# RMS norm and matmul on one core: stores of two tiles from tile 80 on

## The chip, the cores and the metric

One NeuronCore of a Trainium2 chip. The metric is device time in microseconds (us), lower is better. One execution is also taken by the hardware profiler; its trace gives the span from the first to the last instruction.

## The reference: what is computed

```python
batch, seq, dim, out_dim = 16, 1024, 512, 768

def reference(x, gamma, weight, eps):
    rms = np.sqrt(np.mean(x ** 2, axis=-1, keepdims=True) + eps)
    x_norm = x / rms * gamma
    return np.matmul(x_norm, weight).astype(np.float32)
```

All inputs and the output are float32: 16,384 rows of 512 numbers come in (32 MiB), 16,384 rows of 768 go out (48 MiB). Every byte of both has to pass the DMA engines once.

## The kernel before, in words

**Tiles.** The 16,384 rows are cut into `NT` = 128 tiles of 128 rows; a tile has one row on each of the 128 partitions. The main loop takes tiles in pairs `j` (tiles 2j and 2j+1), 64 of them. `gamma` is multiplied into the weights once, which are kept in bf16 (`w_bf`).

**Work on a tile.** GpSimd casts x to bf16 (`cast`, line 188; `cast_quad`, line 260). ScalarE squares each row and sums it (`square`, line 196), takes the root for eight tiles at a time (line 201), and VectorE makes the reciprocal (`rstd`, line 203). PE transposes the tile in words of two bf16 (line 230) and VectorE copies the result out of PSUM (line 239); for 28 of the 128 tiles VectorE transposes 32x32 blocks itself (line 271). PE then multiplies the transposed tile with the weights (line 300), into one of three accumulators in PSUM. `finish_tile` multiplies the accumulator with `rstd` into the output buffer `ot`: ScalarE does even tiles (line 279), VectorE odd ones (line 281).

**Output buffers and stores.** `ot` has three buffers of `OG` = 8 tiles; group g of eight tiles (tiles 8g to 8g+7) uses buffer g % 3. `stretches` gives for every tile the first tile and the size of its store (`o_first`, `o_size`). `store(i)` is called after each tile and issues a DMA on SP's queue only where tile i is the last one of its store (line 293). So a whole group leaves in one DMA of 3 MB, except where `stretches` is told to cut a group: the first one into 1, 1, 2 and 4 tiles, the last but one into 4 and 4, the last into 4, 2 and 2. The output rows are dealt out so that each partition owns neighbouring rows of the output (`rows`): a store of n tiles writes n × 3 KB in one piece from each partition.

**Loads.** x comes in eight tiles at a time (2 MB, 16 KB a partition), into two buffers of 16 tiles. The first 32 tiles are asked for on SP's queue at the start; the rest on ScalarE's queue, one load every four pairs (line 177).

**What sets the order.** The order is written out by hand: every operation is recorded in program order by `Order.add` with the cells that it reads and writes, and `Order.emit` adds the waits from those cells. The cells of `ot` are single tiles, so that the first write to a slot waits for the DMA that last read this slot. In `finish_tile`, the last tile of each store also reads the cell of the tile before it (`before`): VectorE then waits for ScalarE's neighbouring tile, and SP needs to wait for VectorE only.

```python
before = [("ot", s, i % OG - 1)] if i == o_first[i] + o_size[i] - 1 else []
```

Of the kernel before, what the change touches and what calls it, by code (L numbers as in the profile page):

```python
# [100 lines left out]
def kernel(  # L101
# [20 lines left out]
    NT = N // P  # L122
    NP = NT // 2
    XG, OG = 16, 8
    FIRST, START, LEAD = 2 * XG, 4, 14

    def stretches(group, parts):
        first, size, i = {}, {}, 0
        for g in range(NT // group):
            for n in parts.get(g, [group]):  # L130
                for t in range(i, i + n):
                    first[t], size[t] = i, n
                i += n
        return first, size

    last = NT // OG - 1
    x_first, x_size = stretches(OG, {0: [4, 4]})
    o_first, o_size = stretches(OG, {0: [1, 1, 2, 4], last - 1: [4, 4], last: [4, 2, 2]})

    def rows(ap, i, n):  # L140
        base, t = (i - i % OG, OG) if OG <= i < XG else (x_first[i], x_size[i]) if i < OG else (i - i % XG, XG) if i < 2 * XG else (i - i % (2 * XG), 2 * XG)
# [340 lines left out]
```

## Time and profile before

| | us |
|---|---|
| three runs | 208.81, 208.94, 214.95 |
| median | 208.94 |
| profiled execution, its time | 209.01 |
| profiled execution, its span | 207.1 |

DMA issues of the profiled execution (the page's list; bytes and the median time from issue to landing):

```profile
out_dram<-ot SPq DMA_DIRECT2D x13, 3072.0 KB, 22.0
xt<-in_x_dram ACTq DMA_DIRECT2D x12, 2048.0 KB, 19.0
...
out_dram<-ot SPq DMA_DIRECT2D x4, 1536.0 KB, 10.9
out_dram<-ot SPq DMA_DIRECT2D x3, 768.0 KB, 6.7
```

ScalarE's waits (who waited for whom, us in total, times, the longest):

```profile
ACT ot L279 <- PE ps L300: 41.7, 52, 1.9
ACT ot L279 <- DMA out_dram<-ot: 4.2, 3, 1.7
```

How to read the profile: a span is cut into 40 slices, and each digit is the busy share of a slice in tenths (9 is 90% or more). PE is the matmul engine, PEld its weight loads, DVE VectorE, ACT ScalarE, POOL GpSimd, SP the engine that issues stores. The DMA share is the mean over the core's 16 DMA engines. q1 is SP's DMA queue, q10 ScalarE's. A store is split over all 16 DMA engines, eight rows each, and it has landed when the last of the 16 has finished. L279 is line 279 of the kernel.

### The profile page before, as it was taken

How to read it: one execution, taken by the hardware profiler on the slowest of the kernel's cores; microseconds unless marked ns; L12 is line 12 of the kernel's file. 1: busy time of each engine (PE TensorE's matmuls, PEld its weight loads, DVE VectorE, ACT ScalarE, POOL GpSimd, SP SyncE). 2: the span in 40 equal slices, each digit the busy share in tenths (PEclk: the TensorE clock that was granted, in tenths of full speed). 3: DMA queues.
4: the chain of work that ended last, by engine and by line, in shares of the span. 5: the costliest groups of instructions: out<-in, count | busy, mean ns of one | idle time of the engine just before them, and what ended most of it. 6: DMA issues, size and time to landing. Idle time of an engine off the chain costs nothing.

```text
span 207.1 us, 2793 instructions
## 1 busy us (share of the span) xinstructions
PE 196.4 (95%) x1236; PEld 73.1 (35%) x717; DVE 149.4 (72%) x255; ACT 144.6 (70%) x343; POOL 60.0 (29%) x34
## 2 busy tenths in 40 slices
PE   7799999999999999999999999999999999999940
PEld 1233444343344334433333333443344334343310
DVE  0435654999569984999579984999579984999530
ACT  2688899678867787677867877687858768683310
POOL 1437761067003370063403351060702306000000
PEclk9999999999999999999999999999999999999997
DMA  5999999999999999999999999999999999999993
GB/s 208 422 434 449 389 399 418 440 419 432 426 437 435 432 441 419 426 435 432 435 421 427 441 426 427 430 438 424 429 437 426 434 435 435 408 451 387 392 417 125
DMA packets 5920, 85.62 MB, mean 413 GB/s; under 512 B 658, under 2 KB 660, under 8 KB 1556
## 3 DMA queue, kind: packets, MB, share of 16 engines
q1 hardware_dynamic: 4176, 60.29, 68.8%
q10 hardware_dynamic: 1732, 25.17, 28.5%
q8 instruction: 7, 0.11, 0.2%
q14 instruction: 5, 0.04, 0.0%
HBM read 35.13 MB, written 50.33 MB: 413 GB/s over the span
## 4 chain that ended last, share of the span: by engine, by line
PE 92%; DMA 2%; DVE 1%; ACT 1%; issue 0%; SPq 0%
PE ps L300 82%; PE ps L230 10%; DMA xt<-in_x_dram 2%; DVE ot L281 0%; ACT jk L196 0%; DVE xT L239 0%; DVE w_bf L281 0%; ACT rms L201 0%; DVE rstd L203 0%; SPq L477 0%; SPq L436 0%
## 5 line engine op out<-in xcount | busy, mean ns | idle before, releaser
L300 PE MATMUL ps<-w_bf,xT 128*128 128x512 bf16 (+1 forms) x800 | 149.3, 329 | 0.2 <-DVE w_bf L281 0.2
L279 ACT ACTIVATE ot<-ps,rstd 128x768 f32<-128x768 f32 x64 | 57.7, 901 | 47.8 <-PE ps L300 41.7
L196 ACT ACTIVATE jk<-xt 128x512 bf16<-128x512 f32 x128 | 78.7, 618 | 3.1 <-DMA xt<-in_x_dram 3.1
L188 POOL CAST xb<-xt 128x2048 bf16<-128x2048 f32 (+3 forms) x21 | 46.4, 2221 | 113.4 <-PE ps L230 70.1
L281 DVE TENSOR_SCALAR ot<-ps,rstd 128x768 f32<-128x768 f32 x64 | 64.8, 1013 | 8.5 <-PE ps L300 7.8
L296 PEld LDWEIGHTS <-xT 128*128 128x128 bf16 x400 | 39.5, 99 | 60.3 <-issue 52.5
L230 PE MATMUL ps<-ident_f,xb 128*128 128x128 f32 x200 | 54.4, 276 | 1.1 <-POOL xb L188 1.1
L239 DVE COPY xT<-ps 128x1024 bf16<-128x1024 bf16 (+1 forms) x53 | 34.6, 654 | 26.6 <-PE ps L230 24.9
L271 DVE STREAM_TRANSPOSE xTq<-xq 32x256 f32<-32x256 f32 x112 | 48.8, 435 | 3.4
L230 PEld LDWEIGHTS ps<-ident_f,xb 128*128 128x128 f32 x200 | 28.3, 143 | 46.7 <-issue 44.0
L300 PE MATMUL ps<-w_bf,xTq 128*128 128x512 bf16 x224 | 42.8, 326 | 0.0
L196 ACT ACTIVATION_READ_ACCUMULATOR jk<-xt 128x1 f32 x128 | 24.4, 190 | 0.0
L296 PEld LDWEIGHTS <-xTq 128*128 128x128 bf16 x112 | 11.0, 98 | 14.5 <-issue 14.5
L260 POOL CAST xq<-xt 128x2048 bf16<-128x2048 f32 x7 | 13.3, 1897 | 0.0
L203 DVE RECIPROCAL rstd<-rms 128x8 f32<-128x8 f32 (+3 forms) x20 | 3.8, 192 | 7.5 <-ACT rms L201 7.3
L201 ACT ACTIVATE rms<-ssq,eps_sb 128x8 f32<-128x8 f32 (+3 forms) x20 | 6.0, 300 | 0.6
L300 PE MATMUL ps<-warm 128*128 128x512 bf16 x10 | 4.8, 629 | 1.4 <-DVE eps_sb L354 1.4
L279 ACT ACTIVATE w_bf<-w_f,g_sb 128x768 bf16<-128x768 f32 x2 | 1.9, 935 | 1.2 <-DMA w_f<-in_weight_dram 1.2
L377 DVE COPY g_sb<-ps 128x4 f32<-128x4 f32 x1 | 0.2, 163 | 3.2 <-PE ps L371 3.2
L341 ACT ACT_TABLE_LOAD x1 | 1.3, 1283 | 1.5 <-SPq L436 1.5
L281 DVE TENSOR_SCALAR w_bf<-w_f,g_sb 128x512 bf16<-128x512 f32 (+2 forms) x3 | 1.4, 482 | 0.6 <-DMA w_f<-in_weight_dram 0.6
L371 PEld LDWEIGHTS ps<-ident_f,g_row 2*128 2x128 f32 x2 | 0.3, 201 | 2.6 <-issue 2.6
(10 smaller groups left out, 2.0 us busy)
## 6 DMA issues: line engine op xcount, KB each, us to landing
out_dram<-ot SPq DMA_DIRECT2D x13, 3072.0 KB, 22.0
xt<-in_x_dram ACTq DMA_DIRECT2D x12, 2048.0 KB, 19.0
xt<-in_x_dram SPq DMA_DIRECT2D x3, 2048.0 KB, 18.3
out_dram<-ot SPq DMA_DIRECT2D x4, 1536.0 KB, 10.9
out_dram<-ot SPq DMA_DIRECT2D x3, 768.0 KB, 6.7
xt<-in_x_dram SPq DMA_DIRECT2D x2, 1024.0 KB, 7.3
w_f<-in_weight_dram SPq DMA_DIRECT2D x2, 768.0 KB, 7.1
out_dram<-ot SPq DMA_DIRECT2D x2, 384.0 KB, 19.2
```

Of the source, the lines that this page charges most:

```text
L188: run(POOL, lambda: POOL.tensor_copy(out=xb[s][:, i % 8:i % 8 + n, :], in_=src), of, cells("xb", s, i % 8, n))
L196: run(ACT, lambda: ACT.activation(out=jk[j], in_=src[:, 0, :], func=AF.Square, accum_out=ssq[:, i:i + 1]), of, [("jk", j), ("ssq", i)])
L201: run(ACT, lambda: ACT.activation(out=rms[:, s], in_=ssq[:, s], func=AF.Sqrt, scale=1.0 / D, bias=eps_sb), [("ssq", t) for t in range(i, i ...
L203: run(DVE, lambda: DVE.reciprocal(out=rstd[:, s], in_=rms[:, s]), [("rms", i)], [("rstd", t) for t in range(i, i + n)])
L230: run(PE, lambda: PE.transpose(out=tp[b][:, t, h, :], in_=words[:, lo:lo + P], identity=ident_f), cells("xb", s, j % 4 * 2 + t) + ["ident" ...
L239: run(DVE, lambda: DVE.tensor_copy(out=dst[:, t:t + n, :], in_=src[:, t:t + n, :]), [("tp", b)], cells("xT", j % 4, t, n))
L260: run(POOL, lambda: POOL.tensor_copy(out=xq[s], in_=src), of, [("xq", s)])
L271: run(DVE, lambda: DVE.transpose(out=dst, in_=src), [("xq", s)], [("xTq", s)])
L279: run(ACT, lambda: ACT.mul(out=dst, in_=src, mul=r), reads, writes)
L281: run(DVE, lambda: DVE.tensor_single_scalar(out=dst, in_=src, scalar=r, op=mybir.AluOpType.mult), reads, writes)
L296: run(PE, lambda: PE.ldweights(lhsT), [cell])
L300: run(PE, lambda: PE.add_instruction(mybir.InstMatmult(name=nc.get_next_instruction_name(), engine=mybir.EngineType.PE, ins=[PE.lower_ap(r ...
```

## The change

```diff
-    o_first, o_size = stretches(OG, {0: [1, 1, 2, 4], last - 1: [4, 4], last: [4, 2, 2]})
+    o_first, o_size = stretches(OG, {0: [1, 1, 2, 4], **{g: [2, 2, 2, 2] for g in range(NT * 5 // 8 // OG, last + 1)}})
```

`NT * 5 // 8 // OG` is 10 and `last` is 15. So groups 10 to 15 (tiles 80 to 127) are each stored in four DMAs of two tiles, 768 KB, 6 KB a partition: 24 stores. Before, these tiles left in nine stores: groups 10 to 13 whole, group 14 in two of four tiles, group 15 in one of four and two of two. On SP's queue that makes 9 issues of 3 MB and 24 of 768 KB beside the first group's, where it was 13 of 3 MB, 3 of 1.5 MB and 2 of 768 KB. Since each store's last tile waits for the tile before it, every odd tile from 81 on now has that wait, and the waits for free slots of `ot` follow the smaller stores. No other instruction is added, taken away or moved on any engine.

## The prediction

> **What bounds the kernel now.** I read the page's head first: the engines' busy time and the 40 slices.
>
> ```profile
> span 207.1 us, 2793 instructions
> PE 196.4 (95%) x1236; PEld 73.1 (35%) x717; DVE 149.4 (72%) x255; ACT 144.6 (70%) x343; POOL 60.0 (29%) x34
> ...
> DMA  5999999999999999999999999999999999999993
> GB/s 208 422 434 449 389 399 418 440 419 432 426 437 435 432 441 419 426 435 432 435 421 427 441 426 427 430 438 424 429 437 426 434 435 435 408 451 387 392 417 125
> ```
>
> Two resources are full at once: the PE and the 16 DMA engines. So I asked for busy time by stage (columns: stretch; length; busy us and count of PE, PEld, DVE, ACT, POOL; clock; DMA share; GB/s).
>
> ```profile
> 100.00:180.00 80.00, 80.00 (x522) 30.57 (x303) 63.57 (x107) 60.10 (x145) 22.54 (x10) 1.00 1.01 431
> 180.00:190.00 10.00, 10.00 (x67) 3.84 (x38) 9.54 (x18) 5.58 (x14) 0.00 (x0) 1.00 0.99 424
> 190.00:200.00 10.00, 9.11 (x57) 2.64 (x27) 6.08 (x9) 3.60 (x4) 0.00 (x0) 1.00 0.93 390
> 200.00:207.10 7.10, 0.00 (x0) 0.00 (x0) 0.16 (x1) 0.00 (x0) 0.00 (x0) 0.80 0.50 203
> ```
>
> PE never pauses before 198, and from 100 to 180 the DMA engines are full at 431 GB/s. Which ends last? The chain of waits ends with the last VectorE scaling, at 199.15 + 1.02 = 200.17:
>
> ```profile
> 199.15 1.02 DVE ot L281
> ```
>
> That chain follows compute instructions only; the span runs 6.9 us further, to 207.1. The list of DMA issues in the window 200 to 203, and the DMA view of 203 to 207.1, show what fills the rest:
>
> ```profile
> out_dram<-ot SPq DMA_DIRECT2D x1, 768.0 KB, 5.7
> ```
> ```profile
> DMA  6951101010101001010100101000000000000000
> ...
> q1 hardware_dynamic: 45, 0.17, 10.5%
> ```
>
> The last store is issued at 200.46 and lands 5.74 us later, at 206.20, although its 768 KB need under 2 us at 424 GB/s: it queues behind earlier stores. From 203.6 on the digits show one engine in sixteen still moving. In the trace's records of landings, fifteen engines have finished the last store by 204.00 and one finishes at 206.20. This late engine lands the last six stores at 191.22, 195.01, 198.78, 202.50, 204.33 and 206.20. Eight packets of a four-tile store (456 ns each, below) make 3.65 us and those intervals are 3.72 to 3.79, so it hardly rests. **The end is set by the total work of the slowest DMA engine**, plus 0.9 us to the end of the span. The other fifteen are ahead and run dry for moments (0.93 busy in 190 to 200).
>
> **The change, part by part.** Each engine moves 8 of a transfer's 128 rows, one packet a row. Tiles 80 to 127 now leave in 24 stores of 6 KB rows; before it was 9 stores (four of 24 KB rows, three of 12 KB, two of 6 KB). Bytes, loads, and everything before tile 80 stay. PE, VectorE and GpSimd keep their instructions and order.
>
> *More packets.* From the trace's packet records, median length and distance to the next packet of the same engine: 24,576 B take 912 ns, next after 908; 12,288 B 460, next after 456; 6,144 B 234, next after 231. Four 6 KB packets cost 924 where one 24 KB packet cost 908. Per engine:
> - tiles 80 to 111: 4 × 8 × 908 = 29.06 us become 16 × 8 × 231 = 29.57: +0.51
> - tiles 112 to 123: 3 × 8 × 456 = 10.94 become 6 × 8 × 231 = 11.09: +0.14
> - tiles 124 to 127: unchanged
> - 15 more completions, a 4-byte packet of 9 ns each: +0.14
>
> Sum +0.79 us. All of it lies on the path if the late engine never rests, which the change only makes surer, since each pair is issued as soon as it is ready. Lower bound: the late engine needed 7.51 us for the last eight-tile store (0.939 a tile), 0.930 a tile for the last four-tile one and 0.925 for the last two pairs; 44 tiles at 0.925 for 0.94 give −0.6. Upper bound: 6 KB packets in the tail had a mean of 238, not 234; 4 ns on 176 packets add 0.7: +1.5. I take +0.8, the sum over medians, because 6 KB packets beside loads (28 to 42 us) also had a median of 234.
>
> The Trainium skill, page "DMA: Bandwidth & Descriptors", section "Bandwidth", speaks against this change: it asks for at least 1 MiB a DMA, and its table has 341 GB/s there. At that rate a 768 KB store would take 2.3 us (an estimate from the page), and 22 of them for tiles 80 to 123 some 10 us more than now. The trace disagrees where stores queue: the last two pairs land 1.87 us apart, 420 GB/s.
>
> *Issue on SP.* 15 more issues of 0.33 us. SP does nothing else here: it waits for VectorE most of the time (95 us on that one row of its waits). Zero; if several pairs came ready at once the DMA engines would still have a backlog of over 5 us to work on.
>
> *New waits on VectorE.* Every odd tile from 81 now waits for ScalarE's even tile, where only the last of a store did. Queued behind it on VectorE are the 32x32 moves and the PSUM copies that PE needs. ScalarE's scaling ends 0.12 to 1.26 us before VectorE's begins in all but two pairs, 104/105 and 106/107 (−0.08 and 0.01), and there ScalarE itself had waited 1.68 us for a store. Zero; without that cover at most 0.1 us per pair, and PE has three accumulators.
>
> *Buffers and the two queues.* A slot of `ot` is now free when its pair has landed, not its eight. ScalarE waits for stores three times, 4.2 us in all, once 1.69 before tile 96 and once 1.68 before tile 104; the second should vanish. It gains nothing, since PE did not pause there. Against that, loads get ahead: while both queues are full they take turns by packet (36 to 42 us: 16 KB load packets had 55.4% of the engines, 12 KB store packets 43.9%; that is 611 to 460). With 6 KB rows against 16 KB the stores' part falls to 234 / (234 + 611) = 28%. Worst case, loads take everything: small packets come up when the store of tiles 72 to 79 has landed (155.39). Loads still owe the rest of one that lands at 158.04, 2.65 us at 38.6% (their share in 156 to 168) = 1.0, and the last one, 2.10 MB / 431 GB/s = 4.9, so they end at 161.3; tiles 80/81 land near 163.7, 82/83 near 165.5, 84/85 near 167.4. Tiles 104, 106, 108 need them at 165.9 at the earliest, 168 and 170. No one waits: zero. Loads land earlier (the last at 170.47 now), and PE was not waiting for them.
>
> *End.* After the last store all is as before: landing, 0.9 us, end.
>
> **Rivals.**
> - *The late engine catches up.* It is 2.2 us behind the next one at the end, but only 0.2 when the store issued at 143.59 lands; the lag grows while long store packets run. With 6 KB rows it does no worse per tile than the others (0.925 to their 0.93). If growth stops at 0.5, the end moves by 0.8 − 1.7 = −0.9: 208.1. Against: packets of a backlogged engine are where it lost time, whatever their length. Chance 0.15.
> - *6 KB packets are dear when all engines write them.* The top tenth in the tail took 252 to 260 ns. If in the long run of 176 packets that is the rule, +21 ns each add 3.7: 209.0 + 0.8 + 3.7 = 213.5, slower. It decides above some 253 ns a packet (+2%). Against: the medians of 234 in both places where such packets ran. Chance 0.06.
> - *A gap after each store.* If engines paused for each completion, the price is what surrounds a lone transfer: 1.0 us from the first issue to its first packet, 0.5 from the last packet to the landing. 15 × 1.5 = 22: 232. Against: the pairs 1.87 apart leave 0.02 beside 8 × 231. The skill's page puts about 2 us of fixed cost on a DMA (section "Anatomy of one DMA"), of the path issued from GpSimd; here it overlaps. Chance 0.02.
> - *Faster by over 2%* needs 204.8. Compute ends at 200.17; issue at 200.46, then 1.0 to the first packet, 1.85 of packets, 0.5 to land, 0.9, and 1.9 outside the span: 206.6 is the floor without any queue. Only noise gets there: 0.02.
>
> **How the numbers follow.** The profiled execution took 209.01 with a span of 207.1 (1.9 outside it); the median of the three runs is 208.94, so nothing is corrected. Forecast 209.0 + 0.8 = 209.8, chance 0.75 for 208.4 to 210.5 by the bounds. The range takes in the first rival below, and above the beginning of the second: 207.8 to 211.2. Within 2% (204.8 to 213.1, about what a measurement of this kernel can tell from no change) lie the forecast and the first rival: 0.90. Slower 0.08, faster 0.02.
>
> **What would show it.** In the changed profile: more data packets on q1 (tiles 80 to 123 in 22 stores of 128 rows, 2,816, where 7 stores made 896) of about 234 ns; PE full until 198 and the last VectorE scaling within 0.3 us of 200.2; the last load landing some 5 us or more before 170.5; no ScalarE wait before tile 104; the last landing near 207.0, from one late engine. Wrong would be: idle DMA engines before 190, PE pauses after 155, 6 KB packets above 245 ns, or the late engine on time with the rest.

## The result and the profile after

| | before | changed |
|---|---|---|
| median of 12 runs, us | 209.11 | 210.15 |
| ratio (95% interval) | | 1.0047 (1.0029 to 1.0065) |
| profiled execution, its time / span | 209.01 / 207.1 | 210.06 / 208.1 |

The change costs about 1.0 us (0.6 to 1.4), half a per cent. A few executions ran some per cent longer whatever the kernel (214.95 and 213.11 here); the ratios leave them out, and the profile of many_24k below is of such a run, 1.7% above that kernel's fastest. The head of the page of the changed kernel, its 40 slices:

```profile
span 208.1 us, 2803 instructions
...
DMA  5999999999999999999999999999999999999992
GB/s 196 428 435 441 406 385 434 421 437 439 428 433 425 439 433 416 432 435 435 424 430 439 422 430 420 424 427 425 438 390 423 414 421 424 422 425 423 423 426 92
DMA packets 8080, 85.62 MB, mean 411 GB/s; under 512 B 898, under 2 KB 900, under 8 KB 4612
```

The bytes are the same; the last nine full slices lie at 414 to 426 GB/s, where the kernel before went from 451 down to 387 as engines ran dry. Busy time by stage (same columns as before), of the changed kernel twice, then of the kernel before where only its stores of 24 and 12 KB rows run:

```profile
100.00:150.00 50.00, 49.63 (x320) 18.98 (x188) 39.82 (x68) 37.82 (x92) 14.80 (x7) 1.00 1.01 429
```
```profile
165.00:203.00 38.00, 33.24 (x210) 11.71 (x117) 26.54 (x42) 19.95 (x44) 2.94 (x2) 0.99 1.02 424
```
```profile
172.00:190.00 18.00, 18.00 (x120) 7.10 (x70) 14.87 (x26) 11.75 (x28) 2.32 (x2) 1.00 1.00 428
```

Read the last two columns: the engines are full in all three stretches (a share above 1.00 comes from records that overlap: a 6 KB packet is 234 ns long and the next starts after 231). They move 429 GB/s with 24 KB stores and 16 KB loads, and 424 with 6 KB stores alone, where the kernel before moves 428 with longer rows. They are not idle; the same bytes take longer. (PE's 49.63 of 50 is not a pause: the trace holds 1,212 PE records where the same instructions left 1,236 before.)

Loads and stores while both queues are full, 152 to 160 (queue: packets, MB, share of the engines):

```profile
q10 hardware_dynamic: 161, 2.38, 70.2%
q1 hardware_dynamic: 158, 0.96, 28.8%
```

158 packets to 161: the queues take turns packet by packet, so the stores' share falls with their packets, to 28.8%. The last load lands at 163.81, 6.7 us earlier than before, and nobody is faster for it. ScalarE's waits for stores, from its timeline, are these three, before tiles 80, 88 and 96; in the profile before they were before tiles 88, 96 and 104, and the one before tile 104 is gone:

```profile
130.73 0.90 ACT L279 ACTIVATE ot<-ps,rstd 128x768 f32<-128x768 f32 x1 [1.19 <-DMA out_dram<-ot]
...
142.86 0.90 ACT L279 ACTIVATE ot<-ps,rstd 128x768 f32<-128x768 f32 x1 [1.17 <-DMA out_dram<-ot]
...
155.16 0.90 ACT L279 ACTIVATE ot<-ps,rstd 128x768 f32<-128x768 f32 x1 [2.20 <-DMA out_dram<-ot]
```

The end: the last scaling of the chain, the last store (in the list of issues of 200 to 203 it stands with 7.3 us, though it is issued at 199.81), and the DMA view of 204 to 208.1:

```profile
198.49 1.02 DVE ot L281
```
```profile
out_dram<-ot SPq DMA_DIRECT2D x1, 768.0 KB, 7.3
```
```profile
DMA  1422222201101010100101010000000000000000
```

Compute ends 0.65 us earlier than in the trace before (it is ahead by 0.63 at tile 0 already, where nothing was changed), and the last landing comes 0.94 us later, at 207.14. What is late is the DMA engines' work, not the last tile.

### The profile page after: what moved, and what is told of

It is laid out like the page before. It is cut to its first block, busy times and chain, and to the rows that moved or that the text cites. A ratio compares the mean times of both kernels' runs of the same rounds, so it can differ in the third digit from the quotient of the medians.

```text
span 208.1 us, 2803 instructions
## 1 busy us (share of the span) xinstructions
PE 193.4 (93%) x1212; PEld 72.6 (35%) x717; DVE 149.6 (72%) x255; ACT 144.4 (69%) x343; POOL 59.9 (29%) x34
## 4 chain that ended last, share of the span: by engine, by line
PE 90%; DMA 2%; DVE 1%; issue 1%; ACT 1%; SPq 0%
PE ps L300 80%; PE ps L230 10%; DMA xt<-in_x_dram 2%; DVE ot L281 0%; ACT jk L196 0%; DVE xT L239 0%; DVE w_bf L281 0%; ACT rms L201 0%; DVE rstd L203 0%; SPq L477 0%; SPq L436 0%
## 5 line engine op out<-in xcount | busy, mean ns | idle before, releaser
L300 PE MATMUL ps<-w_bf,xT 128*128 128x256 bf16 (+1 forms) x783 | 145.5, 326 | 1.4 <-DVE w_bf L281 0.5
L300 PE MATMUL ps<-w_bf,xTq 128*128 128x256 bf16 (+1 forms) x217 | 41.8, 324 | 0.4
L300 PE MATMUL ps<-warm 128*128 128x512 bf16 x10 | 4.3, 567 | 1.4 <-DVE eps_sb L354 1.4
```

The lines of the kernel that those rows point to most:

```text
L300: run(PE, lambda: PE.add_instruction(mybir.InstMatmult(name=nc.get_next_instruction_name(), engine=mybir.EngineType.PE, ins=[PE.lower_ap(r ...
```

## The experiments

All ratios are against runs of the kernel before on the same chip. For the profiles, the end of the last scaling and the last landing, us:

| kernel | ratio (95%) | last scaling ends | last landing |
|---|---|---|---|
| before, first profile / again | | 200.16 / 200.23 | 206.20 / 206.17 |
| changed, again | 1.0042 (1.0023 to 1.0062) | 200.59 | 206.97 |
| long_6k | 1.0037 (1.0005 to 1.0068) | 201.88 | 206.68 |
| head_pairs | 1.0040 (1.0018 to 1.0063) | 199.93 | 206.75 |
| tail_pairs | 0.9998 (0.9975 to 1.0020) | 200.06 | 206.24 |
| half_pe | 1.0053 (1.0032 to 1.0074) | 197.28 | 208.01 |
| pairs_all | 1.0135 (1.0104 to 1.0167) | 200.21 | 209.34 |
| long_3k_32 | 1.0200 (1.0148 to 1.0252) | 207.71 | 211.76 |
| relief15 | 1.0138 (1.0092 to 1.0185) | 199.97 | 208.26 |
| many_24k | 1.0759 (1.0698 to 1.0820) | 204.60 | 225.10 |

Three theories: *more packets* (the sum of the prediction), *more stores* (a price per store, whatever its packets), *other order* (loads ahead of stores, earlier issue, the new waits).

**long_6k: the packets without the stores.** On the kernel before, a gap (`PAD`) of 16 numbers after every second tile in the buffer:

```diff
-    ot = [sb(f"ot{n}", [P, OG, O], F32) for n in range(3)]
+    ot_flat = [sb(f"ot{n}", [P, (OG // 2) * (2 * O + PAD)], F32) for n in range(3)]
...
+        return buf.rearrange("p (a w) -> p a w", w=2 * O + PAD)[:, t // 2:(t + n) // 2, :2 * O]
...
```

> The nine stores of the kernel before, issued when they were, but the output buffer has a gap of 64 bytes after every second tile from tile 80 on, so that each row leaves in pieces of 6 KB: packets as in the changed kernel, stores and waits as before. Theory 'more packets' (the sum of the prediction): +0.51 and +0.14 us over the kernel before, +0.65, ratio 1.003; the DMA rate falls to about 424 GB/s where only stores run. Rival 'more stores' (each extra store costs the late engine some 0.07 us, whatever its packets): no change, ratio 1.000, 431 GB/s. Rival 'other order' (loads ahead of stores, earlier issue, the new waits on VectorE): loads still get ahead, the waits are gone; no clear change.

Measured: 1.0037, and on one chip a last landing 0.51 after that of before_again (the kernel before, profiled again, below), where the sum says 0.65. From 171 to 189 the engines move 424 GB/s at a share of 1.02, in before_again 430 at 1.00. Nine stores with short packets pay most of the price; 'more stores' at no change falls outside the interval, if narrowly. The waits for stores, here and then in before_again:

```profile
ACT ot L289 <- DMA out_dram<-ot: 11.0, 4, 4.2
...
PE ps L312 <- ACT ot L289: 2.2, 2, 1.9
```
```profile
ACT ot L279 <- DMA out_dram<-ot: 10.2, 4, 3.1
...
PE ps L300 <- ACT ot L279: 0.7, 1, 0.7
```

On this chip the kernel before waits 10.2 us itself, not the 4.2 of its first profile, so the short packets add little to the sum. What they lengthen is the wait before tile 104, from 2.97 to 4.23 us: a slot comes free only when all eight tiles have landed, and the store that frees it now has its short packets beside long loads. PE pauses 2.2 us, and the last scaling ends 1.65 us later than in before_again. The end does not follow: eleven engines land the last store between 205.42 and 205.62, but the slowest, which set the end, are later, up to 206.68.

**many_24k: the stores without the packets.**

```diff
+            parts = n // 2 if first >= 80 else 1
+            for q in range(parts):
+                p0, p1 = P // parts * q, P // parts * (q + 1)
+                order.transfer(SP, lambda p0=p0, p1=p1: SP.dma_start(out=rows(out, first, n)[p0:p1], in_=src[p0:p1]),
+                               reads=cells("ot", s, first % OG, n))
...
```

> The other half alone: 24 stores from tile 80 on with the long packets of before. Each whole group of tiles 80 to 111 leaves in four stores of 32 partitions, each four-tile store in two of 64 partitions, all issued when the one store was. 'More packets': only 15 completions of 9 ns, +0.14 us, ratio 1.001. 'More stores': the whole of the change's cost, +0.8 to +1.0 us, ratio 1.004 to 1.005. A mapping of partitions to engines other than with 128 partitions could add something of its own; then the packets' lengths in the trace tell.

It answers another question. DMA view of 172 to 204, where only such stores run:

```profile
DMA packets 639, 9.56 MB, mean 299 GB/s; under 512 B 196, under 2 KB 196, under 8 KB 196
...
q1 hardware_dynamic: 638, 9.55, 97.4%
```

The engines are busy 97.4% of the time and move 299 GB/s: the packets themselves are slower. In this window those of 24 KB take 1,304 ns in the mean, 916 in the kernel before. The expectation had named that stores of 32 or 64 partitions could do this; why they do is not shown. The Trainium skill, page "SBUF — State Buffer", section "Door 1: The DMA port swizzle", has the reason it would give: 16 ports into the memory, eight partitions each, so that 32 partitions reach only eight of them. The loss of rate agrees; which ports were used no run here shows. As a test of the price per store this run is void.

**pairs_all: the dose.** Groups 1 to 9 in pairs too:

```diff
-    o_first, o_size = stretches(OG, {0: [1, 1, 2, 4], **{g: [2, 2, 2, 2] for g in range(NT * 5 // 8 // OG, last + 1)}})
+    o_first, o_size = stretches(OG, {0: [1, 1, 2, 4], **{g: [2, 2, 2, 2] for g in range(1, last + 1)}})
```

> The change made from tile 8 on: 60 stores of two tiles. 'More packets': for each of the nine more groups 8 x 16 ns and three completions, 0.155 us, so +1.4 on top of the change's 0.8 to 1.0: +2.2 to +2.4 over the kernel before, ratio 1.011. 'More stores' at 0.067 each: 42 more, +2.8, ratio 1.013. 'Other order': with 6 KB against 16 KB rows all along, loads run ahead and stores fall behind early; ScalarE waits for stores more than three times, PE pauses, and the time is more than 4 us longer, ratio above 1.02.

Measured 1.0135, +2.8 us (2.2 to 3.5), last landing 209.34. 'Other order' above 1.02 is excluded; ScalarE waits for stores 6.2 us in all, less than the 10.2 in before_again. Packets and completions give 2.2, the lower edge, so something of the size of 0.6 us remains (by last landings more: 3.17 after before_again, 1.81 of it packets, leaves 1.36). Put on the 42 more stores, 1.36 would be 32 ns each, where the sum has 9, and the number of 'more stores' fits here as well; only the kernels with short packets and unchanged stores speak against it. But the trace has another place for it: the 16 KB load packets, with a median of 611 ns in both, have a mean of 630 here and 618 in before_again, and over 120 of them an engine that is 1.4 us. So a price per store is not shown.

**relief15: does one engine set the end?** On the changed kernel:

```diff
+            cuts = [0, 120, P] if first in (120,) else [0, P]
+            for p0, p1 in zip(cuts, cuts[1:]):
+                order.transfer(SP, lambda p0=p0, p1=p1: SP.dma_start(out=rows(out, first, n)[p0:p1], in_=src[p0:p1]),
+                               reads=cells("ot", s, first % OG, n))
...
```

> The changed kernel, but tiles 120/121 leave in a store of 120 partitions and one of the last 8. The trace tells how many engines each uses; if 120 rows go to 15 engines and 8 rows to 8, one engine has 1.85 us less to do and eight have 0.23 more. If the late engine is the one left out and it alone sets the end: the last landing comes 1.3 us earlier (the next engine is 1.58 ahead of it), 208.7 to 208.9, ratio to the kernel before 0.999. If another engine is the late one: +0.0 to +0.3 against the changed kernel, 210.2 to 210.4. If the end is not set by one engine's work but by the number of stores or by the issue of the last: no gain either, and the sixteen landings of the last store keep their spread of 3.8 us.

The landings show 15 engines on the 120 rows and 8 on the 8, as supposed. But around this store the rate falls, as in many_24k; stretches before it and around it:

```profile
164.00:194.00 30.00, 29.72 (x191) 10.64 (x106) 25.09 (x43) 19.16 (x44) 3.73 (x2) 1.00 1.02 423
195.00:200.00 5.00, 3.91 (x25) 1.07 (x11) 2.04 (x2) 1.80 (x2) 0.00 (x0) 1.00 0.98 358
```

Five microseconds at 358 instead of 423 GB/s are 0.8 us of work more. The kernel is 2.9 us (1.9 to 3.9) above the kernel before, where the changed kernel on this chip is 0.9 above it; the window accounts for only a part. Whether one engine alone sets the end stays open.

**before_again and after_again: two profiles of one chip.**

> The kernel before, profiled on the same chip as the next three, to compare traces of one chip. If the late engine belongs to the kernel, one engine is again some 2 us behind the next at the last store; if it belongs to the chip it was run on, the sixteen landings of the last store have another shape. Time 208.9 to 209.7.

> The changed kernel on the same chip. 'More packets': +0.8 us over the kernel before, ratio 1.003 to 1.005, whether one engine is late or not, with 424 GB/s where only stores run. If the change's cost came from one late engine's dislike of short packets alone, it vanishes where no engine is late: ratio 1.000 to 1.002.

206.97 − 206.17 = 0.80 us between the last landings; the sum was 0.79. That the two agree to 0.01 is luck: the lengths of all packets, a sixteenth of their sum, differ by 0.5 us between the two profiles of the kernel before alone (202.11 and 202.62). When compute starts does not show in the end: tile 0 is scaled 0.73 us later in after_again than in before_again, 0.63 earlier in the first pair, and the last landings are 0.80 and 0.94 apart.

On this chip it is not one engine that is late: in before_again the last store lands on thirteen engines by 204.68 and on the others at 205.51, 205.82 and 206.17. A lone late engine comes and goes with the profile: the slowest is 1.74 us behind the next in head_pairs (another chip) and 1.53 in pairs_all (this chip). What makes it late stays open; the price is about the same with it and without.

**long_3k_32: packets of 3 KB, the stores of before.** As long_6k, with a gap after every tile from tile 32 on:

```diff
-        return buf.rearrange("p (a w) -> p a w", w=2 * O + PAD)[:, t // 2:(t + n) // 2, :2 * O]
+        return buf.rearrange("p (t w) -> p t w", w=O + PAD)[:, t:t + n, :O]
```

> The stores of the kernel before, in number and place, with a gap of 64 bytes after every tile of the output buffer from tile 32 on: rows leave in pieces of 3 KB. A 3,072 B packet's successor comes after 118 ns, so eight cost 944 for 908: 10 groups x 8 x 36 = 2.88 us; three four-tile stores 8 x 16 each, 0.38; two pairs 8 x 5 each, 0.08. 'More packets': +3.3 to +3.5 us, ratio 1.016, with 415 GB/s where only stores run. 'More stores': no change, since there are none. A PE or buffer bound would show as PE pauses and a time beyond +4.5 us.

Measured 1.0200, +4.2 us (3.1 to 5.2). Packets alone give 3.4, which lies inside the interval; 'more stores', no change, is out. The runs behind the ratio fall in two pairs: 212.44 and 212.80, at the price of the packets, and 214.71 and 215.15, some 5.8 us above the kernel before. The profiled run is one of the longer pair, and in it the bound that the expectation named has come in, from the list of waits and the DMA view of 180 to 188:

```profile
ACT ot L288 <- DMA out_dram<-ot: 13.3, 3, 4.8
...
PE ps L311 <- ACT ot L288: 6.3, 3, 2.5
```
```profile
DMA  9999999999999999766312000000000389999999
```

With whole groups of eight behind in the queue, compute waited for slots so long that the last tiles came late (last scaling at 207.71), and near 185 the DMA engines had nearly nothing to do for some 2 us. Here the end does hang on the last tile: its store lands on all sixteen engines within 0.2 us (211.55 to 211.76), 3.7 us after it was issued, where the kernel before takes 5.7. This is the rival in which stores fall behind; of these kernels, only this one, short in packets and whole in groups, shows it.

**half_pe: is PE a bound?** On the changed kernel:

```diff
+            if i >= 8 and k in (1, 2):
+                if feed:
+                    feed()
+                continue
```

> The changed kernel with half of its products: for tiles 8 to 127 the second and third of the four matmul steps of a tile are left out, so PE has some 75 us less to do. If the DMA engines' work sets the end: 209.5 to 210.3, as the changed kernel (up to 1 us less if the start fills sooner). If PE's chain set it, the time would fall until VectorE's 150 us or the DMA bound: at least 5 us less, 205 or below.

```profile
PE 138.7 (66%) x756; PEld 54.4 (26%) x477; DVE 149.7 (72%) x255; ACT 142.0 (68%) x343; POOL 59.9 (29%) x34
...
PE   7799959546729584865949569295875849753400
...
DMA  5999999999999999999999999999999999999991
```
```profile
ACT ot L279 <- DMA out_dram<-ot: 32.2, 9, 4.9
PE ps L300 <- ACT ot L279: 27.4, 12, 4.9
```

PE is busy 58 us less than in the kernel before (75 expected), falls to 66%, and the time is that of the changed kernel (1.0053 to 1.0042, within their intervals). ScalarE now waits 32 us for stores and PE waits for ScalarE: what PE gains, it spends waiting for the DMA engines. The last scaling ends 3.3 us earlier than in after_again; the last landing does not come earlier, but 1.0 us later, for a reason that was not found.

**head_pairs and tail_pairs: the two halves.** Groups 10 to 13 alone in pairs; then groups 14 and 15 alone, everything else as in the kernel before:

```diff
-    o_first, o_size = stretches(OG, {0: [1, 1, 2, 4], last - 1: [4, 4], last: [4, 2, 2]})
+    o_first, o_size = stretches(OG, {0: [1, 1, 2, 4], **{g: [2, 2, 2, 2] for g in range(10, last - 1)}, last - 1: [4, 4], last: [4, 2, 2]})
```
```diff
-    o_first, o_size = stretches(OG, {0: [1, 1, 2, 4], last - 1: [4, 4], last: [4, 2, 2]})
+    o_first, o_size = stretches(OG, {0: [1, 1, 2, 4], **{g: [2, 2, 2, 2] for g in (last - 1, last)}})
```

> Only tiles 80 to 111 in pairs; tiles 112 to 127 as before (4, 4, 4, 2, 2). 'More packets': +0.51 and 12 completions of 9 ns, 0.11: +0.6 us, ratio 1.003; the last landing 0.6 later than the kernel before has on this chip. This part holds the loads that get ahead and the wait before tile 104 that vanishes: if those gained anything, less than +0.6; if loads ahead of stores cost something of their own, more.

> Only tiles 112 to 127 in pairs; groups 10 to 13 whole as before. 'More packets': +0.14 and 3 completions: +0.17 us, ratio 1.001, no difference that can be measured. Issue in finer pieces at the end gains nothing if the late engines work through to the end: the last landing 0.1 to 0.2 later. If the end hung on how soon the last tiles can leave, up to 1 us faster.

Last landings 206.75 and 206.24, 0.55 to 0.58 and 0.04 to 0.07 after the two profiles of the kernel before (206.20 and 206.17; before_again ran on another chip than these two), for sums of 0.62 and 0.17. Finer pieces for tiles 112 to 123 gain nothing; the last two stores are the same in both kernels. In the ratios the halves make +0.8 (0.4 to 1.3) and 0.0 us (−0.5 to 0.4), together the whole within their intervals.

## Why the prediction held, point by point

- **The bound.** Right, and shown: with PE's work cut by 58 us the time stays (half_pe); with compute 1.65 us late the last landing is only 0.51 later, less than the packets alone ask for (long_6k). It has a limit: in the profile of long_3k_32 compute fell so far behind that the end did hang on the last tile.
- **The price of packets.** Right in kind and size: 0.79 predicted, 0.80 between two landings on one chip, 0.94 between the first two profiles, 1.0 (0.6 to 1.4) and 0.9 (0.5 to 1.3) by the ratios. In the changed trace 6 KB packets have a median of 234 ns and a mean of 234.6 from 166 to 203, not the 238 of the upper bound; the rival of dear packets, above 253, is out. The sum has no term for the loads: beside 6 KB stores (150 to 175) their packets have a mean of 630 to 637 ns in the changed kernel's two profiles and in long_6k, 616 in both profiles of the kernel before, which is 0.2 us an engine; in head_pairs, at 618, it is not there.
- **The lower bound and the first rival.** Wrong. In the first changed profile the late engine does not like short packets better: it needs 1.84 to 1.95 us a pair, 1.91 in the median, 0.955 a tile, where its two last pairs before had shown 0.925, and its lag grows from 0.75 (store of tiles 92/93) to 1.58. That it catches up was 0.15 of the chance; it did not.
- **The rule of a least size.** The Trainium skill, page "DMA: Bandwidth & Descriptors", section "Bandwidth", asks for at least 1 MiB a DMA. Here 768 KB stores run at 424 GB/s while others are queued behind them. A gap of 1.5 us after each store did not come.
- **Completions.** 9 ns each was the bare packet. If all that after_again lands later than long_6k (0.29 us for 15 stores) were theirs, it would be 19 ns; the 32 of pairs_all has another candidate, the loads. Too small to matter here, and not settled.
- **New waits on VectorE.** Taken as zero, at most 0.1 a pair. One came of 0.40 us, at tile 97, where ScalarE had waited 2.20 for a store, and in after_again three of 1.6 in all, up to 0.8. Without effect, as the end lies elsewhere.
- **Order of the queues.** 28% predicted, 28.8% seen; no wait for a slot from tile 104 on, as worked out. That the pairs do this is shown on one chip: before tile 104 ScalarE waits 2.97 us in before_again, 4.23 in long_6k with the packets but whole groups, and not at all in after_again. The 4.2 us of waits that the prediction started from were those of one profile; the same kernel had 10.2 in the other, and took as long (209.01 and 209.17).
- **The sign that failed.** The last scaling was to end within 0.3 us of 200.2 and ended at 199.51. Tile 0 was already as much ahead, so this tells nothing of the change.
- **The lone late engine** is not a property of the kernel: before_again and after_again have several. The step "the end is set by the total work of the slowest engine" fits them as well, but that one engine alone sets it in the first profiles was not shown.

## What to carry to other kernels

Where the DMA engines are full from start to end, ask of an edit first what it adds to their work: here each packet cost its bytes and some 5 ns, so rows of 6 KB instead of 24 KB cost 1.8%, and no earlier issue won it back. The chain of waits shows engines only; look at what the queues still hold when it ends. Short packets in one queue hand the bandwidth to the other queue, and if buffers come free by large groups, that can turn into waits of the compute engines (PE paused 6.3 us in long_3k_32, 0.7 in before_again). Before a wait is put down to an edit, profile the kernel before on the same chip: its own waits were 4.2 us in one profile and 10.2 in another.

## What the runs showed of the hardware that was not expected

- The distances from one packet to the next on an engine, 118, 231, 456 and 908 ns for 3, 6, 12 and 24 KB lie on one line: 36.7 ns per 1,000 bytes and 5.3 ns a packet.
- Stores from 32 or 64 partitions, with all sixteen engines at work, ran at 299 GB/s (many_24k), and around one store cut into 120 and 8 partitions the rate fell to 358 for 5 us (relief15); 128 partitions at a time ran at 424 to 431.
- Engines with equal rows of every store end up to 3.8 us apart (203.35 to 207.14 in the changed profile; 202.32 to 208.01 in half_pe), in a pattern that differs from profile to profile, on one chip too.
